# Tile sums shared out differently between array and VectorE at a block's start, norm rows copied by ScalarE, x turned before the projections

## The chip, the cores and the metric

The kernel runs on one core of one Trainium2 chip. The metric is the device time of one execution in microseconds (us), as the median of the runs shown. The program is a chain of matrix products on TensorE (PE), with VectorE (DVE), ScalarE (ACT), GpSimd (POOL) and the queue of SyncE (SP) preparing operands for it.

## The reference

One transformer block for 512 tokens of width 2048. Only its first lines matter here:

```python
sh_a, sc_a, g_a, sh_f, sc_f, g_f = jnp.split(jax.nn.silu(c) @ ada_w[l] + ada_b[l], 6, axis=-1)
h = modulate(rms_norm(x, norm_mix[l]), sh_a, sc_a)      # h * (1 + scale) + shift
proj = h @ w_in[l]
```

The vector `c` (2048 numbers) times the matrix `ada_w` (2048 x 12288) gives shift and scale of every column of `x`. The normalized `x`, scaled and shifted, is `h`; `h` times `w_in` gives the inputs of the convolution and of the attention. Everything behind that (attention, two further large products) is left as it is by the change.

## The kernel before, in words

Widths of 2048 are cut into 16 chunks of 128 columns. The block's beginning works in eight **steps** of two chunks each (`STEP = 2`; step 0 holds chunks 0 and 1, step 7 chunks 14 and 15). A step has two halves that are interleaved with one another by `weave`:

- **Shift and scale** (`start_steps`). The columns of `ada_w` that belong to the step come in eight **tiles** of 128 x 2 x 512 numbers (`araw`, 512 KB each, two transfers by SP per tile, from a ring of ten buffers). Each tile holds two of the 16 **row groups** `k` of the product with `c`. A row group is either multiplied by its number of `c` and added to `acc` by DVE (L345 for the first, L347 for the others), or it is given to PE: four row groups at a time, each as a product with a weight `cz` of 128 x 32 columns, side by side on the four column strips of the array (L341). `SHARE = 4` gives row groups 0 to 3, that is tiles 0 and 1, to PE in every step. Then DVE adds the two sums (L351), PE turns the 4 x 128 result by transposes (L223), and DVE reduces it and adds bias and norm gain (L356, L357, L359): `mod` is ready.
- **Projections** (`start_columns`). ACT makes `ahi` and `h` from the turned `x` (`xnT`) and `mod` (L449), DVE makes `alo = h - ahi` (L452). A weight tile is split into `whi` (ACT, L107) and `wlo` (DVE, L109). Each product then takes three matmuls: `ahi` with `wlo` (L482), `ahi` with `whi` (L483), `alo` with `whi` (L480) for the first 512 columns, 24 in a step; and L115 to L117 for the two further groups of 512 columns ("tokens"), 48 in most steps. Their results are copied (step 0, ACT, L516) or added (DVE, L518). A small product with `wg` (L491, again on 32-column strips) follows in every second step.

Before step 0 can start, `x` is normalized and turned: four diagonal matrices `dg` (one for each 128 tokens, L389, made from sums of squares on ACT and DVE) are multiplied with `x` on PE (L415) and copied to `xnT` by ACT (L417). `turn_x(0, 6)` does chunks 0 to 5 ahead of `mod`; chunks 6 to 15 are turned inside `start_columns(0)`, after `mod` of step 0. The norm gains and biases, loaded as rows (`vrow`, `brow`), are turned by PE (L429) and copied by DVE (L430).

Every engine runs its instructions in its own order. That order is fixed when the program is built; `tc.issue_after(latest[...])` says behind which instruction one may stand. SP and POOL start transfers in order, and a transfer waits for its buffer to be free. Buffers in PSUM: four `main`, four `aux`.

Of the kernel before, what the change touches and what calls it, by code (L numbers as in the profile page):

```python
# [10 lines left out]
F32 = mybir.dt.float32  # L11
# [7 lines left out]
P = 128  # L19
# [53 lines left out]
def block_kernel(ctx: ExitStack, tc: tile.TileContext, a: dict, out: bass.AP):  # L73
# [16 lines left out]
    def note(what):  # L90
        latest[what] = nc.cur_bb.bb.instructions[-1]
# [227 lines left out]
    def start_steps(k0):  # L319
# [5 lines left out]
        acc = accp.tile([P, 512], F32, tag=f"acc{e}", name=f"acc{e}")  # L325
        by_array = range(SHARE)
        raws, pr = [], None
        for ka in range(0, KC, 2):
# [3 lines left out]
            for k in range(ka, ka + 2):  # L332
                w, s = raw[:, k - ka, :], cT[:, k:k + 1]
                if k in by_array:
# [8 lines left out]
                    raws = []  # L343
                elif k == SHARE:
                    nc.vector.tensor_scalar(acc, w, s, None, op0=ALU.mult)  # L345
                else:
                    nc.vector.scalar_tensor_tensor(acc, w, s, acc, op0=ALU.mult, op1=ALU.add)  # L347
# [26 lines left out]
    for i in range(NT):  # L374
# [14 lines left out]
        nc.vector.tensor_scalar(dg, ident, ss, None, op0=ALU.mult)  # L389
        dgs.append(dg)  # L390
    for _ in range(6):
        next(first)
    ENDS = ((CKS, (0, 2, 4, 8, 12, 16)), (CQ, (0, 2, 6, 10, 14, 16)))

    def start_load(k, c0, n):

        raw = (ring[0] if c0 == CKC else aring).tile([P, 2, 512], F32, tag="raw" if c0 == CKC else "araw", name="raw")
        with tc.issue_after(latest["block"]) if k else nullcontext():
            (nc.gpsimd if k else nc.sync).dma_start(raw, rows(w_in, k, STEP, c0, n))
        note("block")  # L400
        return raw.rearrange("p k n -> p (k n)")

    loaded = {CKC: start_load(0, CKC, 512)}

    def start_split(k, c0, n):
        return load_split(ring, None, STEP, n, start_load(k, c0, n) if k else loaded[c0])

    xnT = [act.tile([P, S], F32, tag="alo", name="xnT") for _ in range(KC)]

    def turn_x(ka, kb):  # L410

        pst = [(aux, main)[(k - ka) % 2]() for k in range(ka, kb)]
        for i in range(NT):
# [4 lines left out]

    turn_x(0, 6)
    for _ in range(2):  # L420
        next(first)
    loaded.update({c0: start_load(0, c0, 512) for c0 in (CKS, CQ)})
    wg = sp.tile([P, KC, 32], F32, name="wg")
    note("turned")
    with tc.issue_after(latest["turned"]):
        w0 = start_split(0, CKC, 512)
    for dst, src, n in ((cols, vrow, nrow), (bcol, brow, NB6)):
        ps = aux()
        nc.tensor.transpose(ps[:, :n], src, ident[:n, :n])  # L429
        nc.vector.tensor_copy(dst, ps[:, :n])  # L430
    note("columns")
# [9 lines left out]
    def start_columns(k0):  # L441
        n = STEP
        hs = [sp.tile([P, S], F32, tag="h", name="h", bufs=4) for _ in range(n)]
        hF.extend(hs)
        for k in range(k0, k0 + n):
            hT.append(parts())
        for j in range(2):
            for k in range(k0, k0 + n):
                nc.scalar.activation((hT[k][0], hs[k - k0])[j], xnT[k], AF.Identity, scale=mod[:, 1, k:k + 1],  # L449
                                     bias=mod[:, 0, k:k + 1])  # L450
                if j:
                    nc.vector.tensor_sub(hT[k][1], hs[k - k0], hT[k][0].bitcast(F32))  # L452
        w = start_split(k0, CKC, 512) if k0 else w0
        if k0 == 0:
            with tc.issue_after(latest["block"]):
                nc.gpsimd.dma_start(wg, rows(w_in, 0, KC, CGL, 32))
            note("block")
            turn_x(6, 12)
            turn_x(12, KC)
            ps_kv.extend(main() for _ in range(4))  # L460
            gl_at[0] = aux()
        ps_gl = gl_at[0]
        token = []
# [5 lines left out]
        def split_next():  # L469
            for c0, _, _, k, to in itertools.islice(later, 1):  # L470
                with tc.issue_after(latest["mod"]):
                    to.append(start_split(k, c0, 512))

        for j in range(2):
            for c in range(4):
                cs = slice(c * P, (c + 1) * P)
                for kk in range(n):
# [3 lines left out]
                    else:  # L481
                        nc.tensor.matmul(ps_kv[c], w[1][:, kk, cs], hi, start=k0 + kk == 0, stop=False)  # L482
                        nc.tensor.matmul(ps_kv[c], w[0][:, kk, cs], hi, start=False, stop=False)  # L483
                if j or c % 2:
# [1112 lines left out]
```

## Time and profile before

| | us |
|---|---|
| median of three runs | 2190.26 |
| lowest, highest | 2186.78, 2191.9 |
| the profiled execution | 2186.07 |
| its span (first to last instruction) | 2184.3 |
| PE busy | 2135.7 |
| DVE busy | 1780.6 |
| ACT busy | 1076.4 |

The profile is of one execution. "Busy" of PE counts matmuls with modelled ends, so what tells how closely they follow is the distance between two starts. An fp32 matmul shows as two records (two passes): 4 matmuls of L341 are "x8". The window view gives for each stretch the busy time of each engine with the number of records, the clock that PE was granted, the load of the DMA engines and what they moved. In a timeline row the first number is the start, the second the time from there to the end of the last of the merged records, and the bracket the idle time before it and what ended it.

### The profile page before, as it was taken

How to read it: one execution, taken by the hardware profiler on the slowest of the kernel's cores; microseconds unless marked ns; L12 is line 12 of the kernel's file. 1: busy time of each engine (PE TensorE's matmuls, PEld its weight loads, DVE VectorE, ACT ScalarE, POOL GpSimd, SP SyncE). 2: the span in 40 equal slices, each digit the busy share in tenths (PEclk: the TensorE clock that was granted, in tenths of full speed). 3: DMA queues.
4: the chain of work that ended last, by engine and by line, in shares of the span. 5: the costliest groups of instructions: out<-in, count | busy, mean ns of one | idle time of the engine just before them, and what ended most of it. 6: DMA issues, size and time to landing. Idle time of an engine off the chain costs nothing.

```text
span 2184.3 us, 30547 instructions
## 1 busy us (share of the span) xinstructions
PE 2135.7 (98%) x10989; PEld 1785.3 (82%) x10989; DVE 1780.6 (82%) x2770; ACT 1076.4 (49%) x1803; POOL 241.8 (11%) x314
## 2 busy tenths in 40 slices
PE   6999999999999998999999999999999999999998
PEld 5778778788787786888888888888888878888887
DVE  6988778878878786788888888888888876868787
ACT  4335344554543554745555555555554455544453
POOL 1110000000000133000101110100010021212132
PEclk9999999999999999999999999999999999999999
DMA  9974676545558887546666665665665499998897
GB/s 349 355 264 145 218 230 200 160 142 156 154 179 262 219 176 182 147 138 167 178 164 174 171 166 161 165 166 153 178 163 151 163 258 259 207 234 201 220 185 181
DMA packets 383033, 422.90 MB, mean 194 GB/s; under 512 B 19816, under 2 KB 291472, under 8 KB 382112
## 3 DMA queue, kind: packets, MB, share of 16 engines
q1 hardware_dynamic: 344080, 306.41, 45.0%
q0 software_dynamic: 38800, 114.53, 25.3%
q8 instruction: 86, 1.41, 0.3%
q14 instruction: 67, 0.55, 0.1%
HBM read 385.20 MB, written 19.94 MB: 185 GB/s over the span
## 4 chain that ended last, share of the span: by engine, by line
PE 86%; DMA 7%; DVE 3%; issue 2%; ACT 1%; POOL 1%; SPq 0%; DVEq 0%; ACTq 0%; POOLq 0%
PE main L1293 15%; PE aux L1293 11%; PE aux L1069 11%; PE main L1069 10%; PE main L1295 8%; PE aux L1295 6%; PE main L117 5%; PE main L115 5%; PE main L116 5%; DMA araw<-in_ada_w 3%; PE aux L884 2%; PE aux L856 2%; DMA t<-in_w_out 1%; DMA y<-in_x 1%; DVE acc L347 1%
## 5 line engine op out<-in xcount | busy, mean ns | idle before, releaser
L1293 PE MATMUL main<-hC,whi 128*128 128x512 f32 x1408 | 355.3, 394 | 0.0
L1293 PEld LDWEIGHTS main<-hC,whi 128*128 128x128 f32 x1408 | 253.7, 189 | 46.2 <-DVE hC L1160 0.5
L1293 PE MATMUL aux<-hC,whi 128*128 128x512 f32 x1072 | 268.7, 392 | 0.0
L1293 PEld LDWEIGHTS aux<-hC,whi 128*128 128x128 f32 x1072 | 192.6, 189 | 34.0
L1286 DVE TENSOR_TENSOR wlo<-xy,whi 128x1024 fp32r<-128x1024 f32 x135 | 164.7, 1220 | 62.4 <-ACT whi L1280 62.4
L1280 ACT CAST whi<-xy 128x1024 fp32r<-128x1024 f32 x135 | 141.6, 1049 | 146.8 <-PE main L1293 78.2
L1295 PEld LDWEIGHTS main<-hC,wlo 128*128 128x128 f32 x1408 | 192.2, 190 | 14.3
L1295 PE MATMUL main<-hC,wlo 128*128 128x256 f32 x1408 | 196.2, 282 | 0.0
L1069 PE MATMUL main<-wlo,phi 128*128 128x512 f32 x420 | 165.6, 395 | 10.3 <-DVE wlo L1021 5.2
L1069 PE MATMUL aux<-wlo,phi 128*128 128x512 f32 x420 | 164.2, 391 | 1.7 <-DVE wlo L1021 1.7
L1069 PE MATMUL main<-whi,plo 128*128 128x512 f32 x420 | 165.1, 393 | 0.0
L1069 PE MATMUL main<-whi,phi 128*128 128x512 f32 x420 | 165.0, 393 | 0.0
L1069 PE MATMUL aux<-whi,plo 128*128 128x512 f32 x420 | 163.4, 389 | 0.0
L1069 PE MATMUL aux<-whi,phi 128*128 128x512 f32 x420 | 163.4, 389 | 0.0
L115 PE MATMUL main<-alo,whi 128*128 128x512 f32 x384 | 155.5, 405 | 0.0
L1295 PEld LDWEIGHTS aux<-hC,wlo 128*128 128x128 f32 x1072 | 146.3, 190 | 10.5
L1019 ACT CAST whi<-raw 128x1024 fp32r<-128x1024 f32 x90 | 95.1, 1056 | 114.3 <-PE aux L1069 58.7
L1019 ACT CAST whi<-xy 128x1024 fp32r<-128x1024 f32 x88 | 93.0, 1057 | 118.5 <-PE main L1069 59.6
L117 PE MATMUL main<-ahi,whi 128*128 128x512 f32 x384 | 151.4, 395 | 0.0
L116 PE MATMUL main<-ahi,wlo 128*128 128x512 f32 x384 | 150.7, 392 | 0.0
L1295 PE MATMUL aux<-hC,wlo 128*128 128x256 f32 x1072 | 149.6, 282 | 0.0
L1280 ACT CAST whi<-t 128x1024 fp32r<-128x1024 f32 x84 | 88.3, 1051 | 120.4 <-PE aux L1293 65.2
(347 smaller groups left out, 4442.8 us busy)
## 6 DMA issues: line engine op xcount, KB each, us to landing
xy<-in_ffn_w SPq DMA_DIRECT2D x130, 512.0 KB, 4.8
raw<-in_ffn_w SPq DMA_DIRECT2D x112, 512.0 KB, 4.5
araw<-in_ada_w SPq DMA_DIRECT2D x208, 256.0 KB, 5.0
xy<-in_ffn_w POOLq DMA_DIRECT2D x66, 512.0 KB, 7.5
raw<-in_w_in SPq DMA_DIRECT2D x128, 192.0 KB, 3.5
xy<-in_ada_w SPq DMA_DIRECT2D x80, 256.0 KB, 3.9
graw<-in_ada_w SPq DMA_DIRECT2D x60, 256.0 KB, 2.8
acc<-graw POOLq DMA_DIRECT2D x60, 256.0 KB, 3.8
```

The source lines that it names most:

```text
L115: nc.tensor.matmul(ps, lhs[0], rhs[1], start=first, stop=False)
L116: nc.tensor.matmul(ps, lhs[1], rhs[0], start=False, stop=False)
L117: nc.tensor.matmul(ps, lhs[0], rhs[0], start=False, stop=last)
L347: nc.vector.scalar_tensor_tensor(acc, w, s, acc, op0=ALU.mult, op1=ALU.add)
L856: nc.tensor.matmul(one[b], queries(g, i, h), kT[b][g][:, :L], start=True, stop=True)
L884: nc.tensor.matmul(po[:, b * HD:(b + 1) * HD], s["pT"][b][:, kb * P:(kb + 1) * P], vv[b][:, kb, g * HD:(g + 1) * HD], start=kb == 0, stop= ...
L1019: nc.scalar.copy(hi, wt)
L1069: nc.tensor.matmul(ps, at_k[l][:, tok], wt[r][:, cs], start=begins and m == 0, stop=ends_ and j == i and m == 2, skip_group_check=True)
L1280: nc.scalar.copy(hi, t)
L1286: nc.vector.tensor_sub(lo, t, hi.bitcast(F32))
L1293: nc.tensor.matmul(ps, wt[0][:, ks[k]], hC[p][:, k, :], start=first and k == 0, stop=False, skip_group_check=True)
L1295: nc.tensor.matmul(ps[:, HS:], wt[1][:, ks[k]], hC[p][:, k, 0:HS], start=False, stop=last and k == HK - 1, skip_group_check=True)
```

## The change

- Which row groups go to PE: in step 0 the last four (12 to 15) and no longer the first four; in steps 1, 2 and 3 eight (4 to 7 and 12 to 15); in steps 4 to 7 four (4 to 7).
- The norm gains and biases are copied from PSUM by ACT, and their transposes stand behind the last `dg` (`norms`) in the program.
- All 16 chunks of `x` are turned before `mod` of step 0: six together, then pairs in `main` buffers.
- The weight split is in two parts: the load and `whi` come first (`start_hi`), `wlo` behind `mod` (`start_lo`). The product with `whi` precedes the one with `wlo`.
- The first weight tile of step 1 is loaded by SP and no longer by POOL; `wg` is loaded by SP in step 1 and no longer by POOL at the beginning.

```diff
-        by_array = range(SHARE)
+        by_array = range(12, KC) if not k0 else (*range(4, 8), *range(12, KC)) if k0 in (STEP, 2 * STEP, 3 * STEP) else range(4, 8)
...
-                elif k == SHARE:
+                elif k == 0:
                     nc.vector.tensor_scalar(acc, w, s, None, op0=ALU.mult)
...
+    note("norms")
...
-            (nc.gpsimd if k else nc.sync).dma_start(raw, rows(w_in, k, STEP, c0, n))
+            (nc.gpsimd if k > STEP else nc.sync).dma_start(raw, rows(w_in, k, STEP, c0, n))
...
-    def start_split(k, c0, n):
-        return load_split(ring, None, STEP, n, start_load(k, c0, n) if k else loaded[c0])
+    def start_hi(k, c0, n):
+
+        raw = start_load(k, c0, n) if k else loaded[c0]
+        hi = ring[1].tile([P, 1024], F32R, tag="hi", name="whi")
+        nc.scalar.copy(hi, raw)
+        return raw, hi
+
+    def start_lo(raw, hi):
+
+        lo = ring[2].tile([P, 1024], F32R, tag="lo", name="wlo")
+        nc.vector.tensor_sub(lo, raw, hi.bitcast(F32))
+        return tuple(t.rearrange("p (k n) -> p k n", k=STEP) for t in (hi, lo))
...
-        pst = [(aux, main)[(k - ka) % 2]() for k in range(ka, kb)]
+        pst = [(aux if k < 6 and k % 2 else main)() for k in range(ka, kb)]
...
     turn_x(0, 6)
+    for dst, src, n in ((cols, vrow, nrow), (bcol, brow, NB6)):
+        ps = aux()
+        with tc.issue_after(latest["norms"]):
+            nc.tensor.transpose(ps[:, :n], src, ident[:n, :n])
+        nc.scalar.copy(dst, ps[:, :n])
+    for k in range(6, KC, 2):
+        turn_x(k, k + 2)
...
-    note("turned")
-    with tc.issue_after(latest["turned"]):
-        w0 = start_split(0, CKC, 512)
-    for dst, src, n in ((cols, vrow, nrow), (bcol, brow, NB6)):
-        ps = aux()
-        nc.tensor.transpose(ps[:, :n], src, ident[:n, :n])
-        nc.vector.tensor_copy(dst, ps[:, :n])
+    w0 = start_hi(0, CKC, 512)
...
+        w = start_hi(k0, CKC, 512) if k0 else w0
...
-                if j:
-                    nc.vector.tensor_sub(hT[k][1], hs[k - k0], hT[k][0].bitcast(F32))
-        w = start_split(k0, CKC, 512) if k0 else w0
+        note("h")
+        with tc.issue_after(latest["mod"]):
+            w = start_lo(*w)
+        for k in range(k0, k0 + n):
+            nc.vector.tensor_sub(hT[k][1], hs[k - k0], hT[k][0].bitcast(F32))
         if k0 == 0:
-            with tc.issue_after(latest["block"]):
-                nc.gpsimd.dma_start(wg, rows(w_in, 0, KC, CGL, 32))
-            note("block")
-            turn_x(6, 12)
-            turn_x(12, KC)
             ps_kv.extend(main() for _ in range(4))
             gl_at[0] = aux()
+        elif k0 == STEP:
+            nc.sync.dma_start(wg, rows(w_in, 0, KC, CGL, 32))
...
-                    to.append(start_split(k, c0, 512))
+                    to.append(start_lo(*both))
...
-                        nc.tensor.matmul(ps_kv[c], w[1][:, kk, cs], hi, start=k0 + kk == 0, stop=False)
-                        nc.tensor.matmul(ps_kv[c], w[0][:, kk, cs], hi, start=False, stop=False)
+                        nc.tensor.matmul(ps_kv[c], w[0][:, kk, cs], hi, start=k0 + kk == 0, stop=False)
+                        nc.tensor.matmul(ps_kv[c], w[1][:, kk, cs], hi, start=False, stop=False)
```

Three places show how the instructions move. (In the changed file L415 to L417 are L426 to L428, L429 and L430 are L434 and L435, L107 and L109 are L410 and L416 in this stage, L449 is L462, L452 is L468, L480 to L483 are L494 to L497, L491 is L505, L516 and L518 are L530 and L532.)

**The way to `mod` of step 0.** PE before, from the last turned chunk ahead of `mod` to the first projections; the four `dg` are dg_134, dg_146, dg_157 and dg_169, `acc_171` is the sum of step 0:

```order
L415 MATMUL main<-dg_169,xy 128x128
L223 MATMUL aux<-const,acc_171 128x128 x4
L415 MATMUL aux<-dg_134,xy 128x128 x3
L415 MATMUL aux<-dg_146,xy 128x128 x3
L415 MATMUL aux<-dg_157,xy 128x128 x3
L415 MATMUL aux<-dg_169,xy 128x128 x3
...
L482 MATMUL main<-ahi,wlo 128x512
L483 MATMUL main<-ahi,whi 128x512
```

PE of the change at the same place:

```order
L426 MATMUL main<-dg_157,xy 128x128 x2
L426 MATMUL main<-dg_169,xy 128x128 x2
L341 MATMUL aux<-araw,cz 32x512 x4
L223 MATMUL aux<-const,acc_171 128x128 x4
L496 MATMUL main<-ahi,whi 128x512 x2
L497 MATMUL main<-ahi,wlo 128x512 x2
```

DVE of the change from the last sum of squares to `mod` (before, the rows of dg_169 stood ahead of the first L345, two copies L430 and one L109 between the L347):

```order
L383 TENSOR_REDUCE sh_160<-junk 128x1
L345 TENSOR_SCALAR acc_171<-araw,cT 128x512
L386 TENSOR_TENSOR ss_159<-sh_160 128x1
L347 SCALAR_TENSOR_TENSOR acc_171<-araw,cT,acc_171 128x512
L141 RECIPROCAL ss_159<-ss_159 128x1
L347 SCALAR_TENSOR_TENSOR acc_171<-araw,cT,acc_171 128x512
L389 TENSOR_SCALAR dg_169<-const,ss_159 128x128
L347 SCALAR_TENSOR_TENSOR acc_171<-araw,cT,acc_171 128x512 x9
L351 TENSOR_TENSOR acc_171<-acc_171,aux 128x512
L356 TENSOR_REDUCE mod<-aux 128x2x2
```

On PE all of the turning now stands ahead of the transposes L223, and the array's sums of step 0 stand behind it; on DVE two multiply-adds stand between the last sum of squares and dg_169.

**The array's sums among the projections.** PE before has the four products of a step together; here in step 0, those of step 1:

```order
L480 MATMUL main<-alo,whi 128x512 x2
L341 MATMUL aux<-araw,cz 32x512 x4
L480 MATMUL main<-alo,whi 128x512 x6
L115 MATMUL aux<-wlo,ahi 128x512
L116 MATMUL aux<-whi,alo 128x512
```

PE of the change has eight for step 1: four together at that place, and further on, among the tokens of step 0, two and two:

```order
L117 MATMUL aux<-whi,ahi 128x512
L341 MATMUL aux<-araw,cz 32x512 x2
L115 MATMUL aux<-wlo,ahi 128x512
L116 MATMUL aux<-whi,alo 128x512
L341 MATMUL aux<-araw,cz 32x512 x2
L117 MATMUL aux<-whi,ahi 128x512
```

Counted over steps 1 to 7, PE before has 7 such runs of L341 among the projections; the change has 12 (three each for steps 1 and 2, two for step 3, one each for 4 to 7). Of the runs of L491 (now L505), four before, one is split in two.

**From step 0 to steps 1 and 2.** ACT before, at the end of step 0's tokens and the beginning of step 1:

```order
L516 COPY xy<-aux 128x512 x3
L449 ACTIVATE ahi<-xnT,mod 128x512 x2
L516 COPY xy<-aux 128x512
L449 ACTIVATE h<-xnT,mod 128x512 x2
L107 CAST whi<-raw 128x1024 x2
```

ACT of the change:

```order
L530 COPY xy<-aux 128x512 x6
L462 ACTIVATE ahi<-xnT,mod 128x512
L530 COPY xy<-aux 128x512
L410 CAST whi<-raw 128x1024
L530 COPY xy<-aux 128x512
L462 ACTIVATE ahi<-xnT,mod 128x512
L462 ACTIVATE h<-xnT,mod 128x512 x2
```

PE of the change where step 2's projections begin:

```order
L117 MATMUL aux<-whi,ahi 128x512
L496 MATMUL main<-ahi,whi 128x512 x4
L505 MATMUL aux<-h,wg 32x512 x2
L497 MATMUL main<-ahi,wlo 128x512
L496 MATMUL main<-ahi,whi 128x512
L497 MATMUL main<-ahi,wlo 128x512 x2
```

On ACT the cast of step 1's first weight tile now stands between the last two copies of step 0's tokens, and the second `ahi` behind them. On PE two products with `wg` stand between step 2's first four products and the next. Between the transposes L223 of steps 1 and 2 and the projections of the same step stand 12 matmuls; before, these 12 and a run of L341. Behind step 7 the order of all engines is the same as before.

More of the change, by code (lines that the diff above doesn't have):

```diff
@@ L470, in split_next @@
             for c0, _, _, k, to in itertools.islice(later, 1):
+                with tc.issue_after(latest["h"]) if k0 == 0 else nullcontext():
+                    both = start_hi(k, c0, 512)
                 with tc.issue_after(latest["mod"]):
-                    to.append(start_split(k, c0, 512))
+                    to.append(start_lo(*both))
         for j in range(2):
```

## The prediction, made before the changed kernel was run

> **What bounds the kernel now.** I read the page's totals first, then a window table of the beginning, then the timeline there. The other 2000 us run in the old order, so what the change is worth is how much sooner or later the beginning hands over.
>
> ```profile
> span 2184.3 us, 30547 instructions
> ...
> PE 2135.7 (98%) x10989; PEld 1785.3 (82%) x10989; DVE 1780.6 (82%) x2770; ACT 1076.4 (49%) x1803; POOL 241.8 (11%) x314
> ```
>
> PE is busy for all but 49 us. The stretches:
>
> ```profile
> 12.40:30.00 17.60, 15.49 (x90) 12.16 (x90) 8.78 (x21) 8.31 (x16) 0.00 (x0) 0.90 1.08 359
> 30.00:36.30 6.30, 0.00 (x0) 0.00 (x0) 6.12 (x8) 2.09 (x2) 0.00 (x0) 0.73 1.08 365
> ...
> 43.90:63.30 19.40, 19.40 (x95) 14.22 (x95) 17.52 (x26) 10.08 (x17) 2.14 (x3) 1.00 1.09 357
> ```
>
> From 30 to 36.3 us PE does nothing and DVE works through. From 43.9 us on PE has no gap: there DVE is at 17.5 of 19.4 us and the transfers at 357 GB/s, both nearly full, but PE is what ends last. So an instruction added to PE behind 43.9 us costs its whole time, and whatever lets the projections start sooner is gained whole, as long as operands come. What made PE wait:
>
> ```profile
> 19.51 0.17 DVE L141 RECIPROCAL ss<-ss 128x1 f32<-128x1 f32 x1 [0.36 <-ACT ss L140]
> ...
> 19.71 0.29 DVE L389 TENSOR_SCALAR dg<-const,ss 128x128 f32<-128x128 f32 x1
> ...
> 26.57 0.23 DVE L430 COPY cols<-aux 128x72 f32<-128x72 f32 x1 [3.25 <-PE aux L429]
> ...
> 27.14 2.64 PE L415 MATMUL main<-dg,xy 128*128 128x128 f32 x22
> ...
> 31.35 1.22 DVE L109 TENSOR_TENSOR wlo<-raw,whi 128x1024 fp32r<-128x1024 f32 x1
> ...
> 35.63 0.69 DVE L351 TENSOR_TENSOR acc<-acc,aux 128x512 f32<-128x512 f32 x1
> 36.37 1.11 PE L223 MATMUL aux<-const,acc 128*128 128x128 f32 x4 [6.58 <-DVE acc L351]
> ...
> 37.27 5.82 PE L415 MATMUL aux<-dg,xy 128*128 128x128 f32 x38
> 37.52 0.69 DVE L356 TENSOR_REDUCE mod<-aux 128x4 f32<-128x512 f32 x1 [1.21 <-PE aux L223]
> ...
> 38.44 0.16 DVE L359 SCALAR_TENSOR_TENSOR mod<-mod,cols 128x2 f32<-128x2 f32 x1
> ...
> 38.70 1.52 ACT L449 ACTIVATE ahi<-xnT,mod 128x512 fp32r<-128x512 f32 x2 [2.94 <-DVE mod L359]
> ...
> 43.96 0.48 PE L482 MATMUL main<-ahi,wlo 128*128 128x512 f32 x1
> ```
>
> DVE lost 3.25 us at a copy that waited for PE, and 1.22 us on `wlo`, ahead of its last add at 35.63. Then `mod` was ready at 38.6 us, but the projections began at 43.96, since PE turned the other chunks first.
>
> **The start of the projections.** DVE's copies and its `wlo` go from this path, and four of the 16 row groups are now summed by PE at its end. Two ends have to meet: the sums and the turning. The last `dg` (dg_169) comes later, since one L345 and two L347 stand ahead of it:
>
> ```profile
> L347 DVE SCALAR_TENSOR_TENSOR acc<-araw,cT,acc 128x512 f32<-128x512 f32 x88 | 65.5, 749 | 3.0 <-DMA araw<-in_ada_w 1.6
> ```
>
> Two times 0.75 and about 0.5 us, less the 0.36 us in which DVE waited for ACT's root anyway, and a little for the sooner end of the loads: 20.0 becomes 21.5 us. Behind dg_169 PE has 43 matmuls of the turning, 86 records. The row of 22 records above gives 0.11 us a record, so 9.5 us at full clock: 31.0. DVE is through its 12 row groups by 28.5 us (nine behind dg_169, 0.75 us each). The last tile landed at 30.7 (issued at 24.2, and 6.5 us to landing):
>
> ```profile
> 21.96 2.64 SPq L331 DMA_DIRECT2D araw<-in_ada_w  x4
> ...
> DMA to landing us min/median/max: 5.8/6.5/15.3
> ```
>
> It lands some 2 us sooner, as POOL's 768 KB (`wg`, and step 1's first weights) no longer run ahead of it at 359 GB/s. So **the turning on PE is what ends last**, and ACT's norm copies are free beside it: ACT is busy 8.3 of 17.6 us there.
>
> Next the clock, the fourth number from the right in these stretches:
>
> ```profile
> 16.00:19.20 3.20, 1.37 (x11) 1.13 (x12) 2.82 (x4) 1.17 (x3) 0.00 (x0) 1.00 1.07 371
> 19.20:22.60 3.40, 3.40 (x12) 1.76 (x9) 0.97 (x4) 0.28 (x1) 0.00 (x0) 0.50 1.11 349
> ```
>
> A pause of under 2 us in 3.2 was followed by 3.4 us at half clock. In the change PE runs dry ahead of dg_169:
>
> ```profile
> 16.27 1.16 PE L415 MATMUL main<-dg,xy 128*128 128x128 f32 x8 [0.18 <-DVE dg L389]
> ```
>
> From here it has 11 matmuls (22 records, 2.4 us), to 18.7; then it waits until 21.5, a longer pause than the one above. So I add half of 3.4 us to the turning: 32.7. The array's sums take 1.0 us (33.7; priced below), the add 0.75 (34.5). From L223 to the end of `mod` it was 2.2 us with PE at half clock; at full clock, as in step 1 below, L356 follows L223 by 0.64 and not 1.15 us: 36.3. The first `ahi` takes 0.1 + 0.8: the projections begin at 37.2, 6.7 us sooner than 43.96. Ahead of them PE stands still for 2.3 us and for 0.8 us shortly before; I take one more half-clock stretch, 1.5 us of it inside the projections. **The gain is 5.2 us**, with bounds of 3.7 (two such stretches) and 8.4 (none at either place).
>
> The Trainium skill ("TensorE: Matmul & The Clock Gate", Part 1: The HAM clock gate) says otherwise: the clock falls to half only after at least one idle window of about 3.4 us, in windows that run free of the kernel. By that rule neither pause costs anything and the gain is 8.4 us; the row at 19.20 with its 0.50 speaks against it. It is a rival below.
>
> **The array's further sums.** The price of one run of L341 inside the projections:
>
> ```profile
> 22.76 1.05 PE L341 MATMUL aux<-araw,cz 128*32 128x512 f32 x4
> ...
> 47.73 0.61 PE L480 MATMUL main<-alo,whi 128*128 128x512 f32 x2
> ...
> 48.27 1.07 PE L341 MATMUL aux<-araw,cz 128*32 128x512 f32 x8
> ...
> 49.27 1.66 PE L480 MATMUL main<-alo,whi 128*128 128x512 f32 x6
> ```
>
> Eight L480 stand here from 47.73 to the last one's start at 50.54 (49.27 + 1.66 - 0.39), 2.81 us. Without the run they would take seven times 0.23: 1.61. A run of four costs **1.2 us**. The first row is a run of two matmuls, and it takes 1.05 us as well: side by side on the strips, two last as long as four. The change has 12 such runs where there were 7, and one more of `wg`: six times 1.19 is **7.1 us later**. It takes 12 row groups, 9 us, off DVE, which PE doesn't wait for except at two places:
>
> ```profile
> 88.85 0.66 PE L223 MATMUL aux<-const,acc 128*128 128x128 f32 x4 [0.37 <-DVE acc L351]
> ...
> 133.94 0.50 PE L482 MATMUL main<-ahi,wlo 128*128 128x512 f32 x1 [0.42 <-ACT ahi L449]
> ```
>
> Both go: **0.8 us sooner** (bounds 0 and 1.5, the smaller gaps with them).
>
> **New waits at steps 1 and 2.** A run of L341 used to stand between a step's transposes and its projections; now it stands ahead of both, so these come 1.2 us closer:
>
> ```profile
> 56.89 1.05 ACT L107 CAST whi<-raw 128x1024 fp32r<-128x1024 f32 x1
> ...
> 58.93 0.60 PE L223 MATMUL aux<-const,acc 128*128 128x128 f32 x4
> 59.13 0.59 ACT L516 COPY xy<-aux 128x512 f32<-128x512 f32 x1 [0.71 <-PE aux L117]
> 59.57 0.69 DVE L356 TENSOR_REDUCE mod<-aux 128x4 f32<-128x512 f32 x1
> ...
> 72.73 0.60 PE L223 MATMUL aux<-const,acc 128*128 128x128 f32 x4
> ...
> 76.00 0.15 DVE L359 SCALAR_TENSOR_TENSOR mod<-mod,cols 128x2 f32<-128x2 f32 x1
> ...
> 76.18 1.53 ACT L449 ACTIVATE ahi<-xnT,mod 128x512 fp32r<-128x512 f32 x2 [6.11 <-DVE mod L359]
> ...
> 77.14 0.41 PE L482 MATMUL main<-ahi,wlo 128*128 128x512 f32 x1
> ```
>
> Step 1: PE reaches its projections 3.2 us behind L223 (12 times 0.23 and the transposes). L356 follows at 0.64, `mod` 1.1 behind that, and ACT has the first `ahi` at 2.6; then a copy (0.6), then the cast of step 1's weights (1.05): 4.3. PE waits 1.1 us, and 0.3 more for `wlo` (1.22 on DVE behind the cast): **1.4**. Queued behind the cast on ACT are the last copy, the second `ahi` and `h`; PE needs the former 2 us later and gets it then. Bounds 0 and 2.
>
> Step 2: `mod` came 3.4 us behind L223 and DVE's order there is the same, so the first `ahi` is there at 4.3 and PE waits 1.1 us, where 77.14 was 4.4 behind and just met it. Behind four products stand two of `wg`, which need `h`; ACT makes it behind both `ahi`, 5.7 and 6.5 us behind L223. PE waits 0.5 us, and another 0.7 as the second of the pair comes apart from the first: **2.3**. Bounds 0 and 3.
>
> **The sum.** -5.2 + 7.1 - 0.8 + 1.4 + 2.3 = **+4.8 us**. The profiled execution took 2186.07 us (span 2184.3 and 1.8 around it), so it would take 2190.9; it lies 4.2 us under the median of 2190.26, and on the median I forecast **2195.1**. About 0.2%, 4.4 us, is what a measurement of this kernel can tell from no change; the forecast lies just above that.
>
> **The rivals.**
>
> *The clock stays full* at both pauses: +4.8 - 3.2 = +1.6, 2191.9. This is what the Trainium skill's rule above comes to. For it: such windows may lie otherwise in another execution. Against: the 0.50 row. Chance 0.13.
>
> *The waits of steps 1 and 2 don't come*, because the projections start late enough for ACT or `h` to be ready: 4.8 - 3.7 = +1.1, 2191.4. Against it: the orders are fixed, and both chains begin at L223, which PE issues itself. Chance 0.12.
>
> *The transfers fall behind.* Buffers of tiles that PE sums are free only after its run. In steps 1 to 3 there are twice as many, and their runs stand among the tokens, where DVE had freed them before; I estimate that SP, which starts transfers in order, stops once for some 8 us in a stretch that moved 357 GB/s. The sums of the later steps have time in hand, here for step 4:
>
> ```profile
> 102.81 0.68 DVE L351 TENSOR_TENSOR acc<-acc,aux 128x512 f32<-128x512 f32 x1
> ...
> 108.17 0.60 PE L223 MATMUL aux<-const,acc 128*128 128x128 f32 x4
> ```
>
> 4.7 us, and PE's own delay of about 5 comes to it. What of the 8 us isn't covered, up to 5 us, adds to the forecast: +9.8, 2200.1. It decides from the point where a step's last tile lands behind PE's arrival at its transposes. Chance 0.14.
>
> *Runs of two cost next to nothing.* If two matmuls on strips ran beside their neighbours, the split runs would be free, and 8 whole runs of L341 and 3 of `wg` would stand against 7 and 4: the 7.1 us fall away, -2.3, 2188.0, not slower; with a full clock as well -5.5, faster. It decides at a price of a run of two below about 0.4 us; the 1.05 us of the first L341 row speaks against it. Chance 0.09.
>
> **How the numbers follow.** The forecast has 0.52; the bounds of its terms leave about 0.33 of that above 4.4 us and 0.19 below. Slower by over 0.2%: 0.33 and the third rival, 0.47. Faster: 0.05 of the fourth and 0.02 of the first, with the smaller gaps gone: 0.07. Within 0.2%: the rest, 0.46. The range reaches from 2188.0 (the fourth rival; the first two together give 2188.2) to 2200.1 (the third).
>
> **What would show it.** Right: the first product of step 0's projections near 37 us, with a stretch of 0.50 ahead of or in it; 12 runs of L341 behind it at 1.0 to 1.1 us; a gap on PE of over 1 us ahead of step 1's and step 2's projections, ended by ACT; everything behind step 7 shifted 4 to 5 us later. Wrong: projections that begin below 34 us, runs of two matmuls that take half the time, or gaps later than step 3 that a DMA ended.

## The result, and the profile after

The changed kernel takes 2200.49 us (median of five runs, 2198.15 to 2200.8) where the kernel before, run beside it, takes 2190.26 (median of five runs too, 2186.78 to 2191.9). The ratio is 1.0054, 95% interval 1.0043 to 1.0066: **slower by 0.54%**, 9 to 14 us by the interval. The forecast was 4.8 us slower, 2195.1; the time lies just beyond the upper end of its range, which was its third rival (2200.1). Ratios leave out executions in a second, slower state; in all the runs here only two of e14_last2's eleven (4109.62 and 5217.67 us) were in it, and its median in the table further down counts them in.

The page of the changed kernel, profiled span and busy times (the rows of before stand in the prediction):

```profile
span 2198.9 us, 30586 instructions
...
PE 2145.1 (98%) x11013; PEld 1787.3 (81%) x11013; DVE 1771.3 (81%) x2756; ACT 1075.1 (49%) x1805; POOL 238.2 (11%) x310
```

PE is busy 9.4 us longer (before 2135.7), DVE 9.3 us less; for work alone 7.1 more and 9 less were forecast, and PE's time has products at half clock in it. The span is 14.6 us longer, so PE also stands longer. (The two profiled executions lie further apart than the medians, which are 10.2 us apart: the one of before is quicker than all five timed beside it, the one of the change is the slowest of its five.) The window view of the stretches that were shown of before:

```profile
12.40:30.00 17.60, 15.81 (x111) 15.47 (x112) 12.77 (x25) 11.11 (x24) 0.00 (x0) 1.00 1.07 368
30.00:36.89 6.89, 3.97 (x33) 2.71 (x32) 2.66 (x5) 3.48 (x7) 0.00 (x0) 0.93 1.09 358
36.89:61.00 24.11, 23.45 (x92) 15.99 (x92) 13.59 (x21) 9.67 (x15) 0.00 (x0) 0.88 1.02 315
```

PE now turns all of `x` ahead of the projections, most of it in the first stretch (111 matmul records instead of 90), at full clock. But behind the start of the projections two things are new: the granted clock is 0.88, and the transfers, which had kept 357 GB/s, fall to 315. The way to step 0's projections in the timeline view:

```profile
21.90 0.28 DVE L389 TENSOR_SCALAR dg<-const,ss 128x128 f32<-128x128 f32 x1
22.23 0.49 PE L426 MATMUL main<-dg,xy 128*128 128x128 f32 x2 [1.36 <-DVE dg L389]
...
32.25 1.07 PE L341 MATMUL aux<-araw,cz 128*32 128x512 f32 x8
33.41 0.69 DVE L351 TENSOR_TENSOR acc<-acc,aux 128x512 f32<-128x512 f32 x1 [4.27 <-PE aux L341]
34.15 0.66 PE L223 MATMUL aux<-const,acc 128*128 128x128 f32 x4 [0.84 <-DVE acc L351]
...
36.89 1.22 PE L496 MATMUL main<-ahi,whi 128*128 128x512 f32 x2 [2.08 <-ACT ahi L462]
```

The projections begin at 36.89 us, 7.1 us sooner than before. Where that goes is seen from the first product of each step's projections, read from the timelines (us):

| step | before | changed | later by |
|---|---|---|---|
| 0 | 43.96 | 36.89 | -7.1 |
| 1 | 63.34 | 61.08 | -2.3 |
| 2 | 77.14 | 78.36 | 1.2 |
| 3 | 96.06 | 99.94 | 3.9 |
| 4 | 115.33 | 119.19 | 3.9 |
| 5 | 133.94 | 138.69 | 4.8 |
| 6 | 154.02 | 164.66 | 10.6 |
| 7 | 170.83 | 182.70 | 11.9 |

Up to step 5 this is near the forecast. Then 6 us are lost between the projections of steps 5 and 6, and a little more behind them. The timeline view there, DVE and PE:

```profile
146.83 0.67 DVE L351 TENSOR_TENSOR acc<-acc,aux 128x512 f32<-128x512 f32 x1
147.43 2.31 DVE L347 SCALAR_TENSOR_TENSOR acc<-araw,cT,acc 128x512 f32<-128x512 f32 x3
...
152.43 0.60 PE L223 MATMUL aux<-const,acc 128*128 128x128 f32 x4
...
154.97 0.75 DVE L347 SCALAR_TENSOR_TENSOR acc<-araw,cT,acc 128x512 f32<-128x512 f32 x1 [5.22 <-DMA araw<-in_ada_w]
155.64 0.68 DVE L532 TENSOR_TENSOR xy<-aux,xy 128x512 f32<-128x512 f32 x1
...
156.37 0.79 PE L115 MATMUL aux<-wlo,ahi 128*128 128x512 f32 x1 [3.34 <-DVE xy L532]
...
158.51 1.54 DVE L347 SCALAR_TENSOR_TENSOR acc<-araw,cT,acc 128x512 f32<-128x512 f32 x2 [1.53 <-DMA araw<-in_ada_w]
...
160.57 0.68 DVE L356 TENSOR_REDUCE mod<-aux 128x4 f32<-128x512 f32 x1
...
164.66 0.39 PE L496 MATMUL main<-ahi,whi 128*128 128x512 f32 x1
```

Step 6's own sum is done at 146.83 and PE has transposed it at 152.43: in time. But DVE stands from 149.7 us on at a multiply-add of **step 7**, whose tile has not landed (5.22 us). Queued behind it are the addition of a token (L532), which frees the buffer that PE needs for the next token, so PE stands 3.34 us; and the reduction (L356) that makes `mod` of step 6, which comes 8 us behind its transposes instead of 2.7 as before. The pause also costs clock: from 155.3 to 162.1 us half is granted (0.51 and 0.50 in the window view).

### The profile page after: what moved, and what is told of

It is laid out like the page before. It is cut to its first block, busy times and chain, and to the rows that moved or that the text cites. A ratio compares the mean times of both kernels' runs of the same rounds, so it can differ in the third digit from the quotient of the medians.

```text
span 2198.9 us, 30586 instructions
## 1 busy us (share of the span) xinstructions
PE 2145.1 (98%) x11013; PEld 1787.3 (81%) x11013; DVE 1771.3 (81%) x2756; ACT 1075.1 (49%) x1805; POOL 238.2 (11%) x310
## 2 busy tenths in 40 slices
DMA packets 385400, 422.89 MB, mean 192 GB/s; under 512 B 21864, under 2 KB 293520, under 8 KB 384480
## 4 chain that ended last, share of the span: by engine, by line
PE 85%; DMA 7%; issue 3%; DVE 3%; ACT 1%; POOL 1%; SPq 0%; POOLq 0%; ACTq 0%; DVEq 0%
PE main L1307 14%; PE aux L1083 11%; PE aux L1307 11%; PE main L1083 10%; PE main L1309 7%; PE aux L1309 6%; PE main L117 5%; PE main L115 5%; PE main L116 5%; DMA araw<-in_ada_w 2%; PE aux L898 2%; DMA y<-in_x 2%; PE aux L870 1%; DMA t<-in_w_out 1%; PE aux L115 1%
```

## The experiments

Ratios are to the kernel before as it was timed beside each run, with 95% intervals. All lines of the changed file keep their names here, but for those that an edit moves by one.

| run | time, us | before, us | ratio |
|---|---|---|---|
| e1_four | 2200.80 | 2187.45 | 1.0057 (1.0043 to 1.0070) |
| e2_oldsums | 2187.06 | 2187.45 | 0.9997 (0.9988 to 1.0006) |
| e3_newsums | 2195.08 | 2187.45 | 1.0037 (1.0023 to 1.0050) |
| e4_ring12 | 2190.49 | 2187.45 | 1.0013 (1.0004 to 1.0021) |
| e5_wgpool | 2197.87 | 2188.60 | 1.0043 (1.0030 to 1.0057) |
| e6_old_wgpool | 2189.60 | 2188.60 | 1.0008 (0.9999 to 1.0017) |
| e7_old_wgpool_ring12 | 2191.19 | 2188.60 | 1.0011 (1.0002 to 1.0019) |
| e8_loads_pool | 2193.62 | 2188.60 | 1.0033 (1.0020 to 1.0045) |
| e9_place | 2190.98 | 2188.68 | 1.0013 (1.0004 to 1.0021) |
| e10_before_late | 2193.00 | 2188.68 | 1.0017 (1.0007 to 1.0026) |
| e11_step2 | 2189.48 | 2188.68 | 1.0006 (0.9997 to 1.0015) |
| e12_early | 2189.12 | 2188.68 | 1.0005 (0.9996 to 1.0014) |
| e13_last23 | 2186.09 | 2188.89 | 0.9988 (0.9980 to 0.9997) |
| e14_last2 | 2187.78 | 2188.89 | 0.9992 (0.9982 to 1.0002) |
| e15_both | 2189.64 | 2188.89 | 1.0007 (0.9998 to 1.0016) |

### Which part of the change, and is it buffers

**e1_four**: four row groups by the array in steps 1 to 3.

```diff
-by_array = range(12, KC) if not k0 else (*range(4, 8), *range(12, KC)) if k0 in (STEP, 2 * STEP, 3 * STEP) else range(4, 8)
+by_array = range(12, KC) if not k0 else range(4, 8)
```

> The change with four row groups (4 to 7) by the array in steps 1 to 3, not eight; step 0 keeps its last four. Theory (held buffers: the tiles that PE sums in steps 1 to 3 keep their buffers until PE's run, the transfers fall some 6 us behind, and DVE then waits for step 7's tiles, with step 6's products behind it): five runs of L341 fewer, and no PE gap above 1 us among the tokens of step 5; 2185 to 2190, first product of step 6 not later than in the kernel before (154.0). Rival A (the strip runs cost more than 1.2 us each in themselves, nothing is late): also 2185 to 2190, but the gap of 3.6 us ahead of step 6 stays. Rival B (the moved loads and the turned x delay the transfers, not the sums): 2194 or more, step 7's last tile still issued at 146 or later.

**e2_oldsums**: all but the shares.

```diff
-by_array = range(12, KC) if not k0 else (*range(4, 8), *range(12, KC)) if k0 in (STEP, 2 * STEP, 3 * STEP) else range(4, 8)
+by_array = range(SHARE)
...
-                elif k == 0:
+                elif k == SHARE:
```

> The change with the row groups of before (0 to 3 by the array in every step): all of it but the shared sums. Theory: the turned x gains 4 to 7 us at step 0, the waits at steps 1 and 2 give 0 to 3 back: 2184 to 2189, no late transfers. Rival B (the moved loads delay the transfers): 2194 or more, with a DMA wait of DVE above 2 us in steps 5 to 7. If the gain at the start is not kept by what follows: 2190, and the shift of each step shrinks to 0.

**e3_newsums**: the shares alone, put into the kernel before (the two edits of e2_oldsums the other way round).

> The kernel before with the change's shares of row groups alone (step 0 the last four, steps 1 to 3 eight, steps 4 to 7 the second four), x turned as before. Theory: five runs of L341 more (6 us) and the late transfers (7 us), without the gain at the start: 2199 to 2205. Rival A (runs alone): 2196 to 2198, with no DMA wait of DVE above 2 us ahead of step 6. Rival B: 2196 to 2198 as well, as the loads stand as before.

**e4_ring12**: two buffers more.

```diff
-    aring = pool("araw", 10, stack=st0)
+    aring = pool("araw", 12, stack=st0)
...
+    junks = [ring[2].tile([P, 1024], F32R, tag="lo", name="wlo").bitcast(F32) for _ in range(2)]
...
-            junk = sp.tile([P, D // 2], F32, tag=f"junk{i * m % 2}", name="junk")
+            junk = junks[i * m % 2]
```

> The change with twelve buffers for the tiles instead of ten (the space comes from the scratch tiles of the sums of squares, which take two buffers of the weights' ring, unused at that time). All sums and runs stay. Theory: SP's stops get shorter by what two tiles take (some 3 us), the 3.6 us gap among step 5's tokens and the half clock behind it go: 2193 to 2196, step 6's first product at most 6 us later than before. Rivals A and B: 2199 to 2201, as nothing but the buffers is changed.

Measured: e4_ring12 is 1.0013, so two buffers take away three quarters of the loss, and the gap ahead of step 6 is gone. DVE's instructions stand in the same order in both traces, and no wait of DVE for a tile is left from 36 us to the end of the stage. Buffers it is. But **e1_four fell the other way**: with five runs of L341 fewer it is as slow as the change, and PE's gap in step 5's tokens is still there (4.36 us, where the change has 3.34; the profiled execution is its slowest). So the eight row groups of steps 1 to 3, on which both the theory and the third rival of the prediction rested, are not what holds the buffers. e2_oldsums is neither slower nor faster than before: the shares carry the whole loss, and the gain at the start is lost elsewhere (below). A late tile it has as well, which the theory had excluded: DVE waits 4.40 us for one at 152.25. But there the reduction of step 6 is already done (146.44), and PE loses only 1.14 us ahead of step 6. So a late tile is not enough; it counts what stands behind the instruction that waits for it. e3_newsums is 8 us above the kernel before, which is nearer to the rivals (6 to 8) than to the theory (9 to 15); but DVE waits for tiles there too, by up to 3.7 us, which rival A had excluded.

The view of SP's waits shows who released SP's stops, 60 to 160 us, in the changed kernel:

```profile
SPq L331 <- DMA araw<-in_ada_w: 14.8, 25, 2.1
SPq L331 <- DVE acc L347: 12.0, 10, 3.3
SPq L331 <- DVE wlo L416: 10.1, 4, 6.7
SPq L331 <- PE aux L341: 7.0, 3, 4.2
```

and in e1_four:

```profile
SPq L331 <- DVE acc L347: 19.8, 16, 7.4
SPq L331 <- DVE wlo L416: 17.1, 5, 6.8
SPq L331 <- DMA araw<-in_ada_w: 13.8, 25, 2.3
SPq L331 <- PE aux L341: 1.4, 1, 1.4
```

(Total us, times, longest.) Besides many short stops that end with the landing of a tile, most end with an instruction of DVE, not with PE's run. My reading: DVE stands at a tile that is late, so it frees the next buffer late, so a later tile is late. SP's longest stop in the changed kernel, 6.7 us ahead of step 7's fifth tile, ends when DVE has split a weight tile that lies in the same ring; that split is placed behind `mod` of step 5. The totals alone don't show it, though: in e9_place (below), which is nearly as fast as the kernel before, DVE's L347 and L416 end as much of SP's stops (13.1 and 11.2 us). What is shorter there is the longest single stop (2.0, 3.8, and 1.8 for PE's run).

### `wg` and the moved loads

**e5_wgpool**: `wg` by POOL at the beginning.

```diff
-        elif k0 == STEP:
-            nc.sync.dma_start(wg, rows(w_in, 0, KC, CGL, 32))
+            with tc.issue_after(latest["block"]):
+                nc.gpsimd.dma_start(wg, rows(w_in, 0, KC, CGL, 32))
+            note("block")
```

> The change with wg loaded by POOL at the beginning, as in the kernel before; all else stays. Theory W (wg goes in pieces of 128 bytes: on SP's queue it takes the transfers from 360 to about 243 GB/s from 48 to 56 us, 1 MB or 2.8 us, and SP stands 4.6 us; nothing makes that up later): GB/s from 48 to 56 us at 340 or more, 2194 to 2197, and the 3.6 us gap ahead of step 6 shorter or gone. Theory H (held buffers alone): 2199 to 2201, gap as in the change.

**e8_loads_pool**: the same and step 1's weight tiles by POOL, as before. (The change moves all three of them to SP, not the first alone.)

```diff
-            (nc.gpsimd if k > STEP else nc.sync).dma_start(raw, rows(w_in, k, STEP, c0, n))
+            (nc.gpsimd if k else nc.sync).dma_start(raw, rows(w_in, k, STEP, c0, n))
```

> The change with wg and the three weight tiles of step 1 loaded by POOL, all loads as before. Theory W: as with wg alone, 2194 to 2197. If the three tiles of 512 KB on SP delay the row groups as well: 1 to 3 us below the run with wg alone. Theory H: 2199 to 2201.

The window view, 48 to 56 us, of the changed kernel:

```profile
48.00:52.00 4.00, 4.00 (x18) 2.32 (x16) 0.00 (x0) 1.73 (x3) 0.00 (x0) 1.00 0.87 218
52.00:56.00 4.00, 4.00 (x18) 2.48 (x17) 2.59 (x4) 0.77 (x2) 0.00 (x0) 1.00 0.91 268
```

and of e5_wgpool:

```profile
48.00:52.00 4.00, 4.00 (x18) 1.98 (x15) 1.69 (x3) 0.81 (x2) 0.00 (x0) 1.00 1.08 377
52.00:56.00 4.00, 4.00 (x22) 3.29 (x21) 2.67 (x6) 1.43 (x3) 0.00 (x0) 1.00 1.08 359
```

The hole in the transfers is real and comes from `wg` on SP's queue: 1 MB less in 8 us. But without it the gap ahead of step 6 stays (4.33 us, up to 152.17), and the time falls by little if anything: the interval of 1.0043 overlaps that of the change. So the hole is not what makes the gap. e8_loads_pool is at 1.0033, with an interval that overlaps that of e5_wgpool, and PE still has gaps of 2.76 and 2.26 us behind late tiles; whether the loads' place is worth 2 us is not settled.

### Place or number

In steps 4 to 7 the change gives row groups 4 to 7 to PE, where the kernel before gives 0 to 3. As many, but the run of PE and the multiply-adds of DVE change places in the program.

**e9_place**: the change with 0 to 3 there.

```diff
-by_array = range(12, KC) if not k0 else (*range(4, 8), *range(12, KC)) if k0 in (STEP, 2 * STEP, 3 * STEP) else range(4, 8)
+by_array = range(12, KC) if not k0 else (*range(4, 8), *range(12, KC)) if k0 in (STEP, 2 * STEP, 3 * STEP) else range(4)
...
-                elif k == 0:
+                elif k == (0 if k0 < 4 * STEP else 4):
```

> The change with row groups 0 to 3, not 4 to 7, by the array in steps 4 to 7; steps 0 to 3 as in the change. Theory P (place: with row groups 4 to 7 PE's run for a step stands some 28 matmuls, 7 us, later, behind the first 16 products of the step before and no longer ahead of that step's last tokens; it holds two of ten buffers that much longer, in each of steps 4 to 7): the transfers recover from step 4 on, 335 GB/s or more from 100 to 140 us, the gap of 3.6 us ahead of step 6 below 1 us, 2191 to 2196. Theory N (number: it is the eight row groups of steps 1 to 3 that hold buffers): 2199 to 2201, gap as in the change.

**e10_before_late**: the kernel before with 4 to 7 in steps 4 to 7.

```diff
-        by_array = range(SHARE)
+        by_array = range(SHARE) if k0 < 4 * STEP else range(4, 8)
...
-                elif k == SHARE:
+                elif k == (SHARE if k0 < 4 * STEP else 0):
```

> The kernel before with row groups 4 to 7, not 0 to 3, by the array in steps 4 to 7, and nothing else. Theory P: the same number of runs, each 28 matmuls later; 3 to 8 us slower than before, with a DMA wait of DVE above 2 us and a PE gap above 1.5 us in steps 4 to 7. Theory N: as before within 2 us.

**e12_early**: as many row groups as in the change, but the first ones.

```diff
-by_array = range(12, KC) if not k0 else (*range(4, 8), *range(12, KC)) if k0 in (STEP, 2 * STEP, 3 * STEP) else range(4, 8)
+by_array = range(12, KC) if not k0 else range(8) if k0 in (STEP, 2 * STEP, 3 * STEP) else range(4)
...
-                elif k == 0:
+                elif k == (0 if not k0 else 8 if k0 in (STEP, 2 * STEP, 3 * STEP) else 4):
```

> The change with the first row groups where it has the middle and last: 0 to 7 by the array in steps 1 to 3, 0 to 3 in steps 4 to 7; step 0 keeps 12 to 15. As many matmuls of L341, in whole runs of four and at earlier places. Theory P: no gap ahead of step 6, two runs fewer (2.4 us), 2187 to 2191. Theory N: 2196 to 2200, as eight row groups still hold four buffers.

**e15_both**: the edits of e9_place and of e4_ring12 together.

> The change with row groups 0 to 3 by the array in steps 4 to 7 and twelve buffers for the tiles: both remedies at once. One cause (buffers held too long): as each alone, 0.5 to 4 us above the kernel before. Two causes: the remedies add up, 5 us or more below the kernel before.

Measured: e9_place 1.0013, e12_early 1.0005, e10_before_late 1.0017. **The place decides.** Other row groups for PE in steps 4 to 7, and no fewer of them, take the change from 1.0054 to 1.0013, with all eight of steps 1 to 3 kept. The same edit, put into the kernel before, costs 0.17%, 4 us, with no run added, and brings longer waits: DVE's longest for a tile is 3.63 us (3.10 before), PE's longest gap among the projections 1.62 us, ahead of step 3's (0.42 before). (The 4 us are less than the 9 us which the place costs in the change; what the rest of the change adds to it is not separated.) e15_both is at 1.0007, no better than each remedy alone within the intervals; the two don't add up, which speaks for one cause that either more buffers or the earlier place removes. The timeline of e9_place at the place shown above:

```profile
142.53 0.68 DVE L351 TENSOR_TENSOR acc<-acc,aux 128x512 f32<-128x512 f32 x1
143.13 3.10 DVE L347 SCALAR_TENSOR_TENSOR acc<-araw,cT,acc 128x512 f32<-128x512 f32 x4
...
148.35 0.60 PE L223 MATMUL aux<-const,acc 128*128 128x128 f32 x4
...
149.16 0.68 DVE L356 TENSOR_REDUCE mod<-aux 128x4 f32<-128x512 f32 x1
...
155.50 0.39 PE L496 MATMUL main<-ahi,whi 128*128 128x512 f32 x1
```

DVE has its tiles (it waits 1.26 us for one at 154.36, behind the reduction), the reduction follows the transposes by 0.8 us and not 8, and step 6 begins 1.5 us later than before, where the change was 10.6 late. The transfers, 100 to 160 us (window view): the changed kernel,

```profile
100.00:120.00 20.00, 20.00 (x93) 14.68 (x92) 18.74 (x29) 5.79 (x7) 2.13 (x3) 1.00 1.00 329
120.00:140.00 20.00, 18.70 (x87) 14.01 (x86) 16.31 (x26) 4.36 (x7) 2.12 (x3) 1.00 1.00 326
140.00:160.00 20.00, 16.66 (x74) 11.55 (x73) 13.14 (x20) 3.69 (x5) 4.25 (x6) 0.88 0.88 301
```

and e9_place:

```profile
100.00:120.00 20.00, 20.00 (x93) 14.66 (x92) 18.60 (x28) 6.31 (x8) 2.29 (x4) 1.00 1.04 345
120.00:140.00 20.00, 20.00 (x94) 15.62 (x93) 19.15 (x30) 6.04 (x7) 2.14 (x3) 1.00 1.01 331
140.00:160.00 20.00, 20.00 (x97) 14.68 (x96) 18.33 (x29) 6.09 (x7) 3.55 (x5) 1.00 0.80 284
```

e4_ring12 moves 345, 338 and 242 GB/s. PE is busy throughout in the two remedies (20.00 of 20 us), and 18.70 and 16.66 in the changed kernel. Its transfers are slower in the first two stretches (329 and 326 GB/s) and still move 301 in the last, where the others near their end.

### Where the gain at the start goes with the old shares

**e6_old_wgpool** and **e7_old_wgpool_ring12**: e2_oldsums with `wg` by POOL as in e5_wgpool, and then with the buffers of e4_ring12.

> The change with the row groups of before (0 to 3 in every step) and wg loaded by POOL at the beginning. Theory W: the gap of 4.1 us ahead of step 2's transposes, where PE waited for DVE's add at 68.6, shrinks below 2 us, and the gain of the turned x is kept in part: 2182 to 2185. If DVE's own work is the bound there and not its tiles: the gap stays at 3 to 4 us, 2186 to 2188.

> As the run before, and twelve buffers for the tiles. Theory W: buffers matter little with four row groups by the array, 2181 to 2185. If DVE's own work is the bound: as the run before, within 1 us. If held buffers matter in this variant too: 3 us or more below the run before.

**e11_step2**: e2_oldsums with one run more, in step 2.

```diff
-        by_array = range(SHARE)
+        by_array = range(8) if k0 == 2 * STEP else range(SHARE)
...
-                elif k == SHARE:
+                elif k == by_array[-1] + 1:
```

> All of the change but its sums (row groups 0 to 3 in each step), and in step 2 alone row groups 0 to 7 by the array: one run more. If DVE's own work makes PE wait 4.1 us ahead of step 2's transposes, as I now read the run with the old row groups: the four row groups taken off DVE (3 us) shrink that gap to about 1 us for 1.2 us of PE, 2184 to 2187, below the kernel before. If the tiles of step 2 are late and not DVE: the gap stays, 2188 to 2190.

Three misses. In all three PE stands 2.95 us ahead of step 2's transposes (3.74 in e2_oldsums, which has the hole), with ten or twelve buffers, and in e11_step2 with 3 us less work for DVE. The time of e11_step2 is the one expected for late tiles, but DVE waits for no tile there. The timeline of e11_step2:

```profile
66.05 0.69 DVE L532 TENSOR_TENSOR xy<-aux,xy 128x512 f32<-128x512 f32 x1 [2.69 <-PE aux L117]
...
68.02 1.53 DVE L347 SCALAR_TENSOR_TENSOR acc<-araw,cT,acc 128x512 f32<-128x512 f32 x2
69.58 0.69 DVE L351 TENSOR_TENSOR acc<-acc,aux 128x512 f32<-128x512 f32 x1
...
70.33 0.66 PE L223 MATMUL aux<-const,acc 128*128 128x128 f32 x4 [2.95 <-DVE acc L351]
```

DVE is not overworked; it waits 2.69 us for PE's token, and then three multiply-adds and another token stand ahead of the add, in order, while PE waits for the add. So the last row groups of a step should not be DVE's:

**e13_last23** and **e14_last2** (the edit is shown against e2_oldsums):

```diff
-        by_array = range(SHARE)
+        by_array = (*range(SHARE), *range(12, KC)) if k0 in (2 * STEP, 3 * STEP) else range(SHARE)
```

(in e14_last2 step 2 alone).

> All of the change but its sums; row groups 0 to 3 by the array in each step, and 12 to 15 too in steps 2 and 3. Theory O (order: at a step's end DVE's add stands behind three multiply-adds and two additions of tokens that wait for PE, and PE then waits for it; with the last four row groups by the array nothing stands there): the gaps of 3.3 and 2.3 us ahead of the transposes of steps 2 and 3 go, for 2 to 4 further runs of L341 (2.4 to 4.8 us) on PE: 2184 to 2188. If not the order: gaps stay, 2190 to 2192.

> As the run before, but 12 to 15 by the array in step 2 alone. Theory O: step 2's gap gone, step 3's of 1 to 2.3 us left, 1 or 2 runs of L341 more: 2184 to 2188. If not the order: 2189 to 2191.

The timeline of e13_last23 at the same place:

```profile
67.32 0.69 DVE L351 TENSOR_TENSOR acc<-acc,aux 128x512 f32<-128x512 f32 x1 [2.66 <-PE aux L341]
...
68.06 0.66 PE L223 MATMUL aux<-const,acc 128*128 128x128 f32 x4 [0.36 <-DVE acc L351]
```

Now DVE waits for PE, and PE 0.36 us. e13_last23 takes 2186.09 us, ratio 0.9988 (0.9980 to 0.9997): it is 3 us quicker than the kernel before, at the edge of what can be told, and its interval overlaps that of e2_oldsums: the trace shows that the gap goes; that the time falls with it is not shown beyond the noise. e14_last2 lies between, and can't be told from the kernel before.

## Why the prediction was wrong, point by point

**The start of the projections**: right in its times, in part by luck, and a little short in its gain. Forecast: dg_169 21.5, array's sums from 32.7, `mod` 36.3, projections 37.2; measured 21.90, 32.25, 35.93 and 36.89. The pause ahead of dg_169 cost no clock (1.00 up to 30 us), for which 1.7 us were put in; that dg_169 came 0.4 later, PE began 0.3 behind it, and its 43 matmuls took 10.0 us and not 9.5, made up for most of that. The pause ahead of the projections cost more than forecast; the window view of the changed kernel:

```profile
35.80:39.20 3.40, 2.31 (x6) 1.82 (x7) 3.33 (x6) 3.17 (x5) 0.00 (x0) 0.51 1.10 348
39.20:42.60 3.40, 3.40 (x9) 2.64 (x8) 3.40 (x5) 1.64 (x2) 0.00 (x0) 0.50 1.11 349
```

Two stretches of half clock instead of one, nearly all inside the products. From the first of them to the first product with `alo` it is 6.46 us where it was 3.77: 2.7 us where 1.5 were put in. That product comes at 43.35 where it was 47.73: a gain of 4.4 us, for 5.2 forecast with bounds of 3.7 and 8.4. This term differs between executions: of the eight traces whose kernels begin nearly like the change (the change itself, e1_four, e4_ring12, e5_wgpool, e8_loads_pool, e9_place, e12_early and e15_both), three have two such stretches, three have one (e9_place is one of these), and two have none there (1.00 from 34 to 43 us in e5_wgpool and e15_both). e5_wgpool has the full clock at both pauses, so the first rival (the clock stays full) did not hold in the execution that was profiled, but does in some. The Trainium skill ("TensorE: Matmul & The Clock Gate", Part 1: The HAM clock gate) has the half clock follow at least one idle window of about 3.4 us. The lengths here agree with its windows (6.8 us, two of them); the condition doesn't: in the 3.4 us ahead of the halving at 35.87 PE was idle for 1.9 (0.84 before L223, 1.06 behind it).

**The further runs of PE**: right. Twelve runs, and those of two matmuls cost what those of four do (0.98 and 1.00 us to the next start); the fourth rival fell. In the timeline view of the changed kernel, the next row starts 0.98 us behind:

```profile
50.58 1.05 PE L341 MATMUL aux<-araw,cz 128*32 128x512 f32 x4
51.56 0.50 PE L115 MATMUL aux<-wlo,ahi 128*128 128x512 f32 x1
```

**The waits at steps 1 and 2**: right, a little smaller. In the same view:

```profile
61.08 1.19 PE L496 MATMUL main<-ahi,whi 128*128 128x512 f32 x4 [0.73 <-ACT whi L410]
...
78.36 1.20 PE L496 MATMUL main<-ahi,whi 128*128 128x512 f32 x4 [0.42 <-ACT ahi L462]
79.77 1.75 PE L505 MATMUL aux<-h,wg 128*32 128x512 f32 x4 [0.22 <-ACT h L462]
```

By starts (less the usual 0.23 us) step 1 lost 0.9 us for 1.4 forecast, ended by the cast as said; step 2 lost 0.6 and 0.4, and 0.7 because the divided run of `wg` took 1.7 us, where a run of two of L341 takes 0.98: 1.7 in all for 2.3 forecast. The second rival fell.

**The two old waits of PE** (0.8 us): half right. The one ahead of step 3's transposes went. The one ahead of step 5's projections stands at the same instruction and grew from 0.42 to 1.30 us. The forecast took it for a matter of DVE's work. But the timeline view of the kernel before shows the late tile already:

```profile
132.48 0.49 DVE L345 TENSOR_SCALAR acc<-araw,cT 128x512 f32<-128x512 f32 x1 [3.10 <-DMA araw<-in_ada_w]
132.88 0.15 DVE L359 SCALAR_TENSOR_TENSOR mod<-mod,cols 128x2 f32<-128x2 f32 x1
```

DVE waits 3.10 us for the tile of a multiply-add of step 7, and `mod` of step 5 stands right behind it. In the change the same two instructions stand together (137.24 after a wait of 2.16 us, and 137.64). This is in small what later costs 6 us, and it could be read before the run.

**The sum**: the terms hold up to step 4, and the 4.8 us of step 5 are the forecast's number by luck. At step 4 only four of the five further runs of L341 have passed, since PE's run for steps 4 to 7 stands later; 4.8 less 1.2 is 3.6, and 3.9 was measured. At step 5 the fifth run is still to come, and the late tile's wait fills its place.

**The step that failed** is the one by which the sum has no term for late transfers, the third rival's cover: "The sums of the later steps have time in hand", 4.7 us from step 4's add to its transposes, so that late transfers had the small chance of 0.14. The time in hand shrank but did not run out: from the end of the add to the transposes it is 1.2 us at step 4 and 4.9 us at step 6. But it was that of another instruction. What a late tile stops is DVE's whole queue, and in that queue the multiply-adds of the **next** step stand ahead of this step's reduction and of the tokens that PE needs; these have no time in hand. One of the forecast's own signs of being wrong came with it, a gap later than step 3: on PE it ends with DVE, and DVE's wait with a DMA. That the rival's 2200.1 is so near the time is luck: it put up to 5 us at the transposes, where nothing was lost, and it named the wrong part: the eight row groups of steps 1 to 3 hold buffers, but e1_four without them is as slow, and e9_place and e12_early with them are by 1.0013 and 1.0005 slower than before, a quarter of the loss or less. It was the row groups of steps 4 to 7 (4 to 7 for 0 to 3), which the prediction saw only as a run of PE that stands elsewhere among the products.

What stays open: which of two things makes the tiles late. With the row groups of steps 4 to 7, PE's run moves (28 matmuls later), and DVE's first multiply-adds of a step come earlier in its queue (that of step 7 stands ahead of `mod` of step 5 in the change, behind it in e9_place); no run separates them. The traces narrow it down. Counted from the first product with `alo`, SP issues the tiles of the change and of e9_place at the same times, to 0.1 us, from the fourth tile of step 3 to the last of step 4. They part in step 5: there the change's first two tiles are issued sooner (by 1.0 and 3.0 us) and its third 1.8 us later, behind a stop of 2.7 us that a multiply-add of DVE ends. The one great difference is step 7's fifth tile, 7.4 us later in the change, behind the stop of 6.7 us that DVE's split ends. So both stops speak for DVE; that is read from the traces, not shown by an experiment.

## What to carry to other kernels

Slack belongs to an instruction, not to a result: before calling a transfer covered, list what stands behind its consumer in the same engine's queue, and take the smallest slack among these. Where a ring of buffers is short, as here, the order in which tiles are used and freed can count for more than the amount of work moved; try one or two more buffers first, since they tell at once whether releases are the bound. And look in the trace of before for small waits of the kind that a change could make larger: the 3.10 us at 132.48 stood there. A gain at a stage's start is only kept if every engine that hands over to the critical one in turn (here DVE's add at a step's end) comes sooner too.

## What the runs showed of the hardware

`wg` is 256 KB in pieces of 128 bytes. From SP's queue it took the transfers from 350 to 218 GB/s; the page counts 21864 packets under 512 bytes in the changed kernel. From POOL's queue, where it starts at 8.5 us in e5_wgpool, there was no such hole: 422 GB/s from 8 to 12 us and 355 from 12 to 16, against 424 and 401 in e2_oldsums, which has no `wg` at that time. And the page counts 19816 there, 2048 fewer. The rows, of the changed kernel,

```profile
DMA packets 385400, 422.89 MB, mean 192 GB/s; under 512 B 21864, under 2 KB 293520, under 8 KB 384480
```

and of e5_wgpool:

```profile
DMA packets 383416, 422.89 MB, mean 193 GB/s; under 512 B 19816, under 2 KB 291472, under 8 KB 382496
```

The Trainium skill ("DMA: Bandwidth & Descriptors", Specifications) asks for at least 512 bytes for full rate. The 218 GB/s agree. That the same pieces count as small on one queue and not on the other is what these two rows show; why is not shown.
